# A Strassen–Winograd MLP in another order of its seven products: A12 second, s2 made in the place of s1, other rings for the raw weight blocks

## The chip, the cores and the metric

The kernel runs on one core of one Trainium2 chip. The metric is device time in microseconds of one launch. The kernel before took 734.94 us (median of 3 runs, 733.79 to 735.09). Five engines work in it: TensorE (PE; its weight loads are PEld), VectorE (DVE), ScalarE (ACT), GpSimd (POOL) and SyncE (SP), which issues most transfers. Each engine runs its instructions strictly in its own order; semaphores tie them together.

## The reference

One decoder block in float32 over 512 tokens of width 1024: RMSNorm, an input projection, a pooling mixer and a differential attention mixer, a gated merge and output projection with a residual; cross-attention to 256 memory tokens with a residual; and the MLP, which is what the change touches:

```python
x = x + memory_cross_attention(hc, mem_n, w_cq[l], w_ckv[l], w_co[l])
hm = rms_norm(x, g_mlp[l])                       # D_MODEL 1024, SEQ 512
x = x + jnp.square(jax.nn.relu(hm @ w_up[l])) @ w_down[l]   # D_FF 4096
return rms_norm(x, g_final)
```

## The kernel before

**Float32 by halves.** Every matrix is split into a rounded part and a remainder (`split`: ACT casts the high half, L111; DVE subtracts for the low half, L112), and each product is three matmuls (`mm3`: L105 high by high, L106 high by low, L107 low by high). The right factors lie transposed, 128 rows by 512 tokens.

**Projections.** A projection of width 1024 has 8 output tiles m of 8 x 3 matmuls (128x512). The last one before the MLP is `co` (out of cross-attention). Its tiles run in the order `CO_ORDER` 0 4 1 5 2 6 3 7. `done_co` adds the residual (L573), and `right_factors` makes from tiles m and m+4 the right factors of the MLP's first half: for m < 4, x = g*t (L765, L766, L767), whose halves are B11 and T1; for m >= 4 (L773, L776, L777) the halves B21, B22, T2 and T3; `right_rest` (L791) makes T4. After each tile its square is added to `ss2` (`accumulate`, L263 on ACT, L264 on DVE); when all are there, `ss2` is split (`sp2`) and `stats2`, due `STAT2` steps later, lets PE sum it over the partitions and makes the RMS factor `r2`.

**The MLP's first half** is done in 8 sets n of 512 of the 4096 columns. A set multiplies a 2x2 block matrix by the 2x2 blocks of the right factor with seven block products in the manner of Strassen and Winograd instead of eight. The left factors are the raw blocks A11, A12, A22 and the sums s1 = A21+A22, s3 = A21+A11, s2 = s1+A11 and s4 = s2+A12. A block product is 24 matmuls of 128x256 (`block_product`). `up_set` adds the results in PSUM (tag `sc`, 3 banks) to running sums in SBUF (`plus`, L885), and `squared_relu` (L860, L861, then `split`) turns C11, C12, C21, C22 into right factors for the second half. The result of s1 stays in its bank (`u["P5"]`) until that of s3 is there. Two sets are followed by eight tiles of the second half (`dn`).

**Loads.** `load` fetches a raw block of 128x1024 (512 KB) on SP. s1 and s3 are added in flight: SP fetches one block, then POOL issues an accumulating transfer on top (L164, L167). s2 and s4 are additions on DVE (`combined`, L182 and L185). Raw blocks lie in two rings: `wraw` with 3 buffers, which all other weights use too, and `mraw` with 5, which exists only once the first part's buffers are given back (`renew`, during the first tiles of `co`). `prep` splits a block into a pair of halves (`whi`/`wlo`, 3 pairs, or `mhl`, 2 pairs).

**Order.** PE's order is that of the program. The order on the other engines is made by a scheduler that places instructions by a priority and by its own timeline; `tc.high_priority()` raises it for a block of code. In `done_co` this is done for the last two tiles, 3 and 7.

Of the kernel before, what the change touches and what calls it, by code (L numbers as in the profile page):

```python
# [14 lines left out]
ALU = mybir.AluOpType  # L15
AX = mybir.AxisListType

P = 128
# [14 lines left out]
MEMIN, EARLY, LATE = 16, [4, 5, 6, 0, 1], [2, 7, 3]  # L33
WARM = 8
ON_POOL = (1, 3, 5, 7), (1, 3, 5)
STAT1, STAT2, STATM = 16, 13, 20
CO_ORDER = 0, 4, 1, 5, 2, 6, 3, 7
PARTS = "A11", "A12", "A21", "A22"
ORDER = "A11", "s2", "s1", "s3", "A12", "A22", "s4"
FIRST_ORDER = "A11", "s1", "s2", "A12", "s3", "A22", "s4"  # L40
PLAN = "q0 k0 q1 k1 q2 q3 g4 k2 g5 g6 k3 g7 u0 u1 u2 u3 g0 g1 g2 g3"

G_MIX, G_CROSS, G_MEM, G_MLP, G_FINAL, PSCALE, GSUB, LAMS = 0, 8, 16, 24, 32, 40, 44, 45
# [7 lines left out]
def block_kernel(ctx: ExitStack, tc: tile.TileContext, x0g, xT, memT, wv, wm, wst, wckv, wpool, vecs, csts, outT):  # L51
# [24 lines left out]
    def sb(tag, shape, bufs, dt=F32):  # L76
        p = apool if tag in EARLY_TAGS else late["pool"] if tag in LATE_TAGS else pool
        return p.tile(shape, dt, tag=tag, name=nm(tag), bufs=bufs)
# [67 lines left out]
    def fetch(key, src, tag, bufs):  # L146
        if key not in raw:
            raw[key] = sb(tag, [P, D], bufs)
            nc.sync.dma_start(raw[key], src)
        return raw[key]  # L150

    def part(n, name):
        return wst[4 * n + PARTS.index(name)]

    def load(i):
        if i >= len(blocks):
            return
        if isinstance(blocks[i], tuple):
            n, name = blocks[i]
            if (n, "A11") not in raw:  # L160
                fetch((n, "A11"), part(n, "A11"), "mraw", 5)
            if (n, "s1") not in raw and name in ("s1", "s2"):
                r = fetch((n, "s1"), part(n, "A22"), "wraw", 3)
                nc.gpsimd.dma_start(r, part(n, "A21"), accum_op=ALU.add)  # L164
            if (n, "s3") not in raw and name == "s3":
                r = fetch((n, "s3"), part(n, "A21"), "mraw", 5)
                nc.gpsimd.dma_start(r, part(n, "A11"), accum_op=ALU.add)  # L167
            if name in ("A12", "A22"):
                fetch((n, name), part(n, name), "mraw", 5)
        elif i == 0 and i not in raw:  # L170
            r = raw[i] = sb("wraw", [P, D], 3)
            nc.sync.dma_start(r[:, :T], blocks[i][:, :T])
            load_x(1)
            nc.sync.dma_start(r[:, T:], blocks[i][:, T:])
        else:
            fetch(i, blocks[i], "wraw", 3)

    def combined(n, name):

        if name == "s2":  # L180
            r = raw[n, "s2"] = sb("wraw", [P, D], 3)
            V.tensor_tensor(r, raw[n, "s1"], raw[n, "A11"], op=ALU.add)  # L182
        elif name == "s4":
            r = raw[n, "s2"]
            V.tensor_tensor(r, r, raw[n, "A12"], op=ALU.add)  # L185
            return r
        return raw[n, name]

# [609 lines left out]
    def done_co(m, o):  # L798
        with tc.high_priority() if m in CO_ORDER[-2:] else nullcontext():
            residual(m, o)  # L800
            right_factors(m, res[m])
        accumulate(ss2, m, res[m])
        if m == KC - 1:
            for r in rest:
                right_rest(*r)
# [5 lines left out]
        late["pool"] = ctx.enter_context(tc.tile_pool(name="late", bufs=1))  # L811

    projection("co", cross_o, [0, 1, 2, 3, 4, 5], [6, 7], done_co, renew, CO_ORDER)
    sp2 = split_sq(ss2, T)

    def stats2():
        st["r2"] = rstd_full(sp2, ss2)
# [56 lines left out]
    def up_set(n, act, j0):  # L874

        x, y = ((pair("xg", 8), pair("xg", 8)) for _ in range(2))
        for i in range(2):
            act[j0 + i] = (x[0][:, i, :], x[1][:, i, :])
            act[j0 + 2 + i] = (y[0][:, i, :], y[1][:, i, :])
        u = {}  # L880

        def plus(new, o, old):
            if new not in u:
                u[new] = tmp()
            V.tensor_tensor(u[new], o, u[old], op=ALU.add)  # L885

        for name in FIRST_ORDER if n == 0 else ORDER:
            o = ps("sc", 3)
            block_product(W(n, name), right[RIGHT[name]], o)
            if name == "A11":  # L890
                u["P1"] = tmp()
                S.copy(u["P1"], o)
            elif name == "s2":
                plus("U2", o, "P1")
            elif name == "s1":
                u["P5"] = o
            elif name == "s3":
                plus("U3", o, "U2")
                plus("C22", u["P5"], "U3")
                u["U4"] = u["U2"]  # L900
                plus("U4", u["P5"], "U2")
                squared_relu(*y, u["C22"], B, ALU.min)
            elif name == "A12":
                u["C11"] = u["P1"]
                plus("C11", o, "P1")
                squared_relu(*x, u["C11"], A)
            elif name == "A22":
                u["C21"] = u["U3"]
                plus("C21", o, "U3")
                squared_relu(*y, u["C21"], A, ALU.min)  # L910
            elif name == "s4":
                u["C12"] = u["U4"]
                plus("C12", o, "U4")
                squared_relu(*x, u["C12"], B)
# [110 lines left out]
```

## Time and profile before

| what | us |
|---|---|
| median of 3 runs | 734.94 |
| the profiled execution, its time | 733.65 |
| its span, first to last instruction | 731.7 |
| PE busy in it | 706.8 (97%) |
| DVE busy | 512.7 (70%) |
| ACT busy | 392.4 (54%) |

The page gives busy times by engine, the span in 40 slices, the transfers, the chain of waits that ended last, and the costliest groups of instructions. The timeline gives each instruction with its start, its duration and, in square brackets, the idle time of its engine before it and what ended it. The view by windows gives the busy time of each engine in a stretch, the count of its instructions, the TensorE clock granted by the throttle (1.00 is full) and the share of time in which the 16 DMA engines were busy. A line such as L112 is that of a helper, so the tile's name says what is meant.

### The profile page before, as it was taken

Reading aid. Unit: us, or ns where it says so; the run is one execution under the profiler, and the core shown is the slowest. Engines: PE = TensorE matmul, PEld = TensorE weight load, DVE = VectorE, ACT = ScalarE, POOL = GpSimd, SP = SyncE. Lnnn points to the kernel's source line nnn. Section 1 sums busy time; section 2 is a strip of 40 time slices with the busy share of each in tenths; the row PEclk is TensorE's granted clock in tenths of the full one; section 3 lists DMA queues with packets and bytes.
Section 4 is the critical chain, followed back from the end, with each engine's and each line's share of the span. In section 5 each row is a group of like instructions: output and inputs, shape, how many; then the busy total and the mean of one; then the engine's idle time right before and its main releaser. Section 6 shows DMA issues by size and latency. Waiting matters only on the chain.

```text
span 731.7 us, 10275 instructions
## 1 busy us (share of the span) xinstructions
PE 706.8 (97%) x3960; PEld 614.1 (84%) x3960; DVE 512.7 (70%) x797; ACT 392.4 (54%) x641; POOL 72.6 (10%) x66
## 2 busy tenths in 40 slices
PE   9999999999999999999969999999999999999993
PEld 6877888788889888888849988899889988899882
DVE  7597999975888555663887974588455974489426
ACT  7498998676766433543754641256214651256422
POOL 0044112534000000000000001000000001000003
PEclk9999999999999999999988999999999999999997
DMA  8433223143525542114734646265354645314003
GB/s 318 142 114 117 78 82 115 59 142 119 173 91 186 187 141 87 58 58 159 187 86 122 197 143 144 86 173 184 77 115 146 202 144 118 83 58 144 30 1 115
DMA packets 28112, 91.09 MB, mean 124 GB/s; under 512 B 3072, under 2 KB 5120, under 8 KB 28064
## 3 DMA queue, kind: packets, MB, share of 16 engines
q1 hardware_dynamic: 25712, 81.92, 33.9%
q0 software_dynamic: 2352, 8.52, 6.9%
q8 instruction: 31, 0.51, 0.3%
q14 instruction: 17, 0.14, 0.1%
HBM read 86.24 MB, written 2.10 MB: 121 GB/s over the span
## 4 chain that ended last, share of the span: by engine, by line
PE 81%; DVE 6%; DMA 5%; ACT 5%; issue 1%; POOL 0%; SPq 0%; DVEq 0%; POOLq 0%; ACTq 0%
PE acc L105 16%; PE acc L107 15%; PE acc L106 15%; PE sc L105 10%; PE sc L107 10%; PE sc L106 10%; DMA wraw<-wst 3%; DMA mraw<-wst 2%; DVE wlo L112 1%; ACT tmp L448 1%; ACT whi L111 1%; DVE mix L849 1%; DVE tmp L446 1%; DMA tmp<-xT 1%; PE sc L387 1%
## 5 line engine op out<-in xcount | busy, mean ns | idle before, releaser
L111 ACT CAST whi<-wraw 128x1024 fp32r<-128x1024 f32 (+1 forms) x98 | 102.4, 1045 | 118.1 <-PE acc L106 50.8
L105 PE MATMUL acc<-xg,whi 128*128 128x512 f32 x400 | 158.2, 396 | 0.0
L107 PE MATMUL acc<-xg,wlo 128*128 128x512 f32 x400 | 156.1, 390 | 0.0
L106 PE MATMUL acc<-xg,whi 128*128 128x512 f32 x400 | 155.8, 390 | 0.0
L112 DVE TENSOR_TENSOR wlo<-wraw,whi 128x1024 fp32r<-128x1024 f32 (+1 forms) x98 | 121.3, 1238 | 27.7 <-ACT whi L111 27.4
L107 PEld LDWEIGHTS acc<-xg,wlo 128*128 128x128 f32 x400 | 75.1, 188 | 16.1
L105 PEld LDWEIGHTS acc<-xg,whi 128*128 128x128 f32 x400 | 75.2, 188 | 15.0 <-issue 0.3
L106 PEld LDWEIGHTS acc<-xg,whi 128*128 128x128 f32 x400 | 75.2, 188 | 14.5
L573 DVE TENSOR_TENSOR vr<-acc,vr 128x512 f32<-128x512 f32 x41 | 28.3, 690 | 72.3 <-PE acc L107 72.3
L105 PE MATMUL sc<-mix,whi 128*128 128x256 f32 (+1 forms) x192 | 56.8, 296 | 0.0
L107 PE MATMUL sc<-mix,wlo 128*128 128x256 f32 (+1 forms) x192 | 56.4, 294 | 0.0
L106 PE MATMUL sc<-mix,whi 128*128 128x256 f32 (+1 forms) x192 | 56.4, 294 | 0.0
L885 DVE TENSOR_TENSOR tmp<-sc,tmp 128x512 f32<-128x512 f32 x56 | 37.7, 686 | 7.5 <-PE sc L107 7.3
L111 ACT CAST mhl<-wraw 128x1024 fp32r<-128x1024 f32 x22 | 23.2, 1053 | 35.6 <-PE acc L106 22.2
L111 ACT CAST whi<-mraw 128x1024 fp32r<-128x1024 f32 x19 | 19.9, 1050 | 38.6 <-PE acc L106 21.8
L106 PE MATMUL acc<-xg,mhl 128*128 128x512 f32 x104 | 40.6, 390 | 0.0
L105 PE MATMUL acc<-xg,mhl 128*128 128x512 f32 x104 | 40.5, 389 | 0.0
L107 PE MATMUL acc<-xg,mhl 128*128 128x512 f32 x104 | 40.5, 389 | 0.0
L105 PEld LDWEIGHTS sc<-mix,whi 128*128 128x128 f32 x192 | 36.5, 190 | 1.0
L106 PEld LDWEIGHTS sc<-mix,whi 128*128 128x128 f32 x192 | 36.4, 189 | 1.1
L107 PEld LDWEIGHTS sc<-mix,wlo 128*128 128x128 f32 x192 | 36.4, 190 | 1.1
L167 POOL DMA_DIRECT2D mraw<-wst x8 | 6.9, 864 | 263.5 <-DMA mraw<-wst 164.3
(270 smaller groups left out, 1684.9 us busy)
## 6 DMA issues: line engine op xcount, KB each, us to landing
wraw<-wm SPq DMA_DIRECT2D x76, 512.0 KB, 3.3
mraw<-wst SPq DMA_DIRECT2D x32, 512.0 KB, 3.4
wraw<-wckv SPq DMA_DIRECT2D x16, 512.0 KB, 3.4
mraw<-wst POOLq DMA_DIRECT2D x8, 512.0 KB, 5.7
wraw<-wst SPq DMA_DIRECT2D x8, 512.0 KB, 3.3
wraw<-wst POOLq DMA_DIRECT2D x8, 512.0 KB, 5.6
s<-s SPq DMA_DIRECT2D x8, 256.0 KB, 3.6
vr<-xT SPq DMA_DIRECT2D x8, 256.0 KB, 4.4
```

Of the source, the lines that this page charges most:

```text
L105: nc.tensor.matmul(o, lh, rh, start=start, stop=False)
L106: nc.tensor.matmul(o, lh, rl, start=False, stop=False)
L107: nc.tensor.matmul(o, ll, rh, start=False, stop=stop)
L111: S.copy(hi, src)
L112: eng.tensor_tensor(lo, src, f(hi), op=ALU.subtract)
L167: nc.gpsimd.dma_start(r, part(n, "A11"), accum_op=ALU.add)
L387: nc.tensor.matmul(o[i], xg[k][0][:, tb], wh[:, c], start=k == 0, stop=False)
L446: V.tensor_tensor_reduce(e[:, :n], o[:, :n], mask[:, T - n:], -0.125, 3.0e38, ALU.add, ALU.min, mn)
L448: S.activation(e[:, :n], e[:, :n], AF.Exp, bias=mn, scale=-1.0, accum_out=sm[:, c:c + 1])
L573: V.tensor_tensor(t, o, t, op=ALU.add)
L849: eng.tensor_tensor(y3[j][:, i, c], y3[j][:, i, c], r, op=ALU.mult)
L885: V.tensor_tensor(u[new], o, u[old], op=ALU.add)
```

## The change

The seven products of a set run in the order A11 A12 s1 s2 s3 A22 s4; before, it was A11 s2 s1 s3 A12 A22 s4. In the first set it is A11 s1 A12 s2 s3 A22 s4; before, A11 s1 s2 A12 s3 A22 s4. s2 is formed on DVE in the buffer of s1, where before it had one of its own. The raw s1 moves from the ring `wraw` to the ring `mraw`, and the raw A12 and A22 move from `mraw` to `wraw`. The additions of the squares of the last two `co` tiles and the split of their sum are at high priority too. `STAT2` is 11, before 13. C11 gets a buffer of its own, since A12 is now multiplied while P1 is still needed.

```diff
--- before.py
+++ after.py
@@ -33,11 +33,11 @@
 MEMIN, EARLY, LATE = 16, [4, 5, 6, 0, 1], [2, 7, 3]
 WARM = 8
 ON_POOL = (1, 3, 5, 7), (1, 3, 5)
-STAT1, STAT2, STATM = 16, 13, 20
+STAT1, STAT2, STATM = 16, 11, 20
 CO_ORDER = 0, 4, 1, 5, 2, 6, 3, 7
 PARTS = "A11", "A12", "A21", "A22"
-ORDER = "A11", "s2", "s1", "s3", "A12", "A22", "s4"
-FIRST_ORDER = "A11", "s1", "s2", "A12", "s3", "A22", "s4"
+ORDER = "A11", "A12", "s1", "s2", "s3", "A22", "s4"
+FIRST_ORDER = "A11", "s1", "A12", "s2", "s3", "A22", "s4"
 PLAN = "q0 k0 q1 k1 q2 q3 g4 k2 g5 g6 k3 g7 u0 u1 u2 u3 g0 g1 g2 g3"
 
 G_MIX, G_CROSS, G_MEM, G_MLP, G_FINAL, PSCALE, GSUB, LAMS = 0, 8, 16, 24, 32, 40, 44, 45
@@ -157,16 +157,13 @@
             return
         if isinstance(blocks[i], tuple):
             n, name = blocks[i]
-            if (n, "A11") not in raw:
-                fetch((n, "A11"), part(n, "A11"), "mraw", 5)
-            if (n, "s1") not in raw and name in ("s1", "s2"):
-                r = fetch((n, "s1"), part(n, "A22"), "wraw", 3)
-                nc.gpsimd.dma_start(r, part(n, "A21"), accum_op=ALU.add)
-            if (n, "s3") not in raw and name == "s3":
-                r = fetch((n, "s3"), part(n, "A21"), "mraw", 5)
-                nc.gpsimd.dma_start(r, part(n, "A11"), accum_op=ALU.add)
-            if name in ("A12", "A22"):
-                fetch((n, name), part(n, name), "mraw", 5)
+            if name in ("s1", "s3"):
+                first, then = ("A22", "A21") if name == "s1" else ("A21", "A11")
+                if (n, name) not in raw:
+                    r = fetch((n, name), part(n, first), "mraw", 5)
+                    nc.gpsimd.dma_start(r, part(n, then), accum_op=ALU.add)
+            elif name in PARTS:
+                fetch((n, name), part(n, name), "mraw" if name == "A11" else "wraw", 5 if name == "A11" else 3)
         elif i == 0 and i not in raw:
             r = raw[i] = sb("wraw", [P, D], 3)
             nc.sync.dma_start(r[:, :T], blocks[i][:, :T])
@@ -177,12 +174,9 @@
 
     def combined(n, name):
 
-        if name == "s2":
-            r = raw[n, "s2"] = sb("wraw", [P, D], 3)
-            V.tensor_tensor(r, raw[n, "s1"], raw[n, "A11"], op=ALU.add)
-        elif name == "s4":
-            r = raw[n, "s2"]
-            V.tensor_tensor(r, r, raw[n, "A12"], op=ALU.add)
+        if name in ("s2", "s4"):
+            r = raw[n, "s1"]
+            V.tensor_tensor(r, r, raw[n, "A11" if name == "s2" else "A12"], op=ALU.add)
             return r
         return raw[n, name]
 
@@ -799,7 +793,7 @@
         with tc.high_priority() if m in CO_ORDER[-2:] else nullcontext():
             residual(m, o)
             right_factors(m, res[m])
-        accumulate(ss2, m, res[m])
+            accumulate(ss2, m, res[m])
         if m == KC - 1:
             for r in rest:
                 right_rest(*r)
@@ -811,7 +805,8 @@
         late["pool"] = ctx.enter_context(tc.tile_pool(name="late", bufs=1))
 
     projection("co", cross_o, [0, 1, 2, 3, 4, 5], [6, 7], done_co, renew, CO_ORDER)
-    sp2 = split_sq(ss2, T)
+    with tc.high_priority():
+        sp2 = split_sq(ss2, T)
 
     def stats2():
         st["r2"] = rstd_full(sp2, ss2)
@@ -901,7 +896,6 @@
                 plus("U4", u["P5"], "U2")
                 squared_relu(*y, u["C22"], B, ALU.min)
             elif name == "A12":
-                u["C11"] = u["P1"]
                 plus("C11", o, "P1")
                 squared_relu(*x, u["C11"], A)
             elif name == "A22":
```

The scheduler's order changes with it. On DVE, from the residual of tile 3 of `co` (`vr_1890`) to the low half of its right factor (`mix_3594`), which is the last that the product A11 needs, before (`wraw_3825` is s2 of the second set, `wraw_3670` first s2 and then s4 of the first):

```order
L573 TENSOR_TENSOR vr_1890<-acc_3560,vr_1890 128x512
L112 TENSOR_TENSOR wlo_3673<-wraw_3670,whi_3672 128x1024
L182 TENSOR_TENSOR wraw_3825<-wraw_3711,mraw_3668 128x1024
L112 TENSOR_TENSOR s_3548<-tmp_3545,s_3548 128x512
L767 TENSOR_TENSOR tmp_3593<-tmp_3593,tmp_3595 128x256
L185 TENSOR_TENSOR wraw_3670<-wraw_3670,mraw_3661 128x1024
L264 TENSOR_TENSOR ss_3244<-ss_3244,tmp_3601 128x512
L573 TENSOR_TENSOR vr_1898<-acc_3604,vr_1898 128x512
L791 SCALAR_TENSOR_TENSOR tmp_3545<-tmp_3545,tmp_3542 128x256
L112 TENSOR_TENSOR wlo_3677<-mraw_3661,whi_3676 128x1024
L112 TENSOR_TENSOR mix_3594<-tmp_3593,mix_3594 128x512
```

The same stretch of DVE in the changed kernel (its line numbers are lower by 5 or 6; `mraw_3561` is s1, from here on s2, of the first set, `wraw_3605` is A12):

```order
L567 TENSOR_TENSOR vr_1890<-acc_3560,vr_1890 128x512
L112 TENSOR_TENSOR wlo_3671<-wraw_3605,whi_3670 128x1024
L785 SCALAR_TENSOR_TENSOR tmp_3545<-tmp_3545,tmp_3542 128x256
L761 TENSOR_TENSOR tmp_3593<-tmp_3593,tmp_3595 128x256
L258 TENSOR_TENSOR ss_3244<-ss_3244,tmp_3601 128x512
L112 TENSOR_TENSOR s_3554<-tmp_3545,s_3554 128x256
L567 TENSOR_TENSOR vr_1898<-acc_3604,vr_1898 128x512
L112 TENSOR_TENSOR wlo_3676<-mraw_3561,whi_3675 128x1024
L112 TENSOR_TENSOR mix_3594<-tmp_3593,mix_3594 128x512
```

The two additions of 1024 columns (`wraw_3825`, `wraw_3670`) have left the stretch, `s_3548` now stands just ahead of it, and `s_3554` has come in.

On POOL, the first four accumulating transfers before: s3 of the first and of the second set, then s1 of the first and of the second.

```order
L167 DMA mraw_3663<-wst 128x1024
L167 DMA mraw_3775<-wst 128x1024
L164 DMA wraw_3561<-wst 128x1024
L164 DMA wraw_3711<-wst 128x1024
```

And in the changed kernel: s1 and s3 of the first set, then s1 and s3 of the second.

```order
L164 DMA mraw_3561<-wst 128x1024
L164 DMA mraw_3663<-wst 128x1024
L164 DMA mraw_3741<-wst 128x1024
L164 DMA mraw_3822<-wst 128x1024
```

s1 has moved ahead of s3; its buffer `mraw_3561` is now one of the five that SP fills first when the ring `mraw` comes into being.

On ACT, between the square of tile 3 (`tmp_3601`) and the high half of its right factor (`mix_3594`), before:

```order
L263 ACTIVATE tmp_3601<-vr_1890 128x512
L111 CAST whi_3676<-mraw_3661 128x1024
L111 CAST mix_3594<-tmp_3593 128x512
L773 ACTIVATE tmp_3634<-vr_1898,vx_67 128x512
L111 CAST s_3554<-tmp_3545 128x256
```

and in the changed kernel (`whi_3675` is the high half of s2, before it was that of A12):

```order
L257 ACTIVATE tmp_3601<-vr_1890 128x512
L111 CAST s_3554<-tmp_3545 128x256
L111 CAST whi_3675<-mraw_3561 128x1024
L111 CAST mix_3594<-tmp_3593 128x512
L767 ACTIVATE tmp_3636<-vr_1898,vx_67 128x512
```

`s_3554` has moved ahead; a cast of a weight block still stands right ahead of `mix_3594`.

## The prediction, made before the change was run

> **What bounds the kernel now.** First the page:
>
> ```profile
> span 731.7 us, 10275 instructions
> PE 706.8 (97%) x3960; PEld 614.1 (84%) x3960; DVE 512.7 (70%) x797; ACT 392.4 (54%) x641; POOL 72.6 (10%) x66
> ```
>
> PE is the bound. An edit on other engines pays only where PE stands still or runs at a lower clock, so I asked the view by windows where that is (columns: us, PE busy, PEld, DVE, ACT, POOL, granted clock, DMA share, GB/s):
>
> ```profile
> 54.00:58.00 4.00, 2.42 (x13) 2.02 (x13) 2.63 (x5) 2.24 (x5) 2.56 (x2) 1.00 0.62 186
> 336.00:375.00 39.00, 39.00 (x173) 32.06 (x172) 28.73 (x45) 23.31 (x38) 3.46 (x4) 1.00 0.70 193
> 376.40:378.50 2.10, 0.00 (x0) 0.00 (x0) 1.04 (x1) 0.32 (x1) 0.00 (x0) 1.00 0.21 39
> 378.50:378.70 0.20, 0.00 (x0) 0.00 (x0) 0.20 (x2) 0.00 (x0) 0.00 (x0) 0.71 0.00 0
> 384.09:388.70 4.61, 4.61 (x21) 4.61 (x22) 3.53 (x8) 2.05 (x3) 0.00 (x0) 0.50 0.35 114
> 388.70:389.00 0.30, 0.30 (x4) 0.30 (x3) 0.30 (x1) 0.30 (x2) 0.00 (x0) 0.80 0.00 0
> 410.00:700.00 290.00, 290.00 (x1827) 262.60 (x1826) 193.30 (x230) 123.13 (x152) 9.48 (x11) 1.00 0.44 124
> ```
>
> From 410 to 700, where nearly all of the eight sets lie, PE is busy without a gap: the new order of products can gain nothing there, only lose. The gap that the change can touch lies at the first product, between `co` and the MLP. There the clock also falls to 0.50 and stays so for 4.6 us after PE is back at work. PE's timeline there:
>
> ```profile
> 374.70 0.39 PE L106 MATMUL acc<-xg,whi 128*128 128x512 f32 x1
> 374.93 0.39 PE L107 MATMUL acc<-xg,wlo 128*128 128x512 f32 x1
> 375.15 0.28 PE L105 MATMUL sc<-mix,mhl 128*128 128x256 f32 x1
> 376.10 0.28 PE L107 MATMUL sc<-mix,mhl 128*128 128x256 f32 x1
> 380.33 0.58 PE L105 MATMUL sc<-mix,mhl 128*128 128x256 f32 x1 [3.95 <-ACT mix L111]
> 384.09 0.58 PE L106 MATMUL sc<-mix,mhl 128*128 128x256 f32 x1 [3.18 <-DVE mix L112]
> ...
> 388.90 0.28 PE L107 MATMUL sc<-mix,wlo 128*128 128x256 f32 x1
> 390.67 0.28 PE L107 MATMUL sc<-mix,wlo 128*128 128x256 f32 x1
> 390.78 0.28 PE L105 MATMUL sc<-s,whi 128*128 128x256 f32 x1
> ```
>
> A11 starts at 375.15, does the nine matmuls of k = 0 to 2, and then lacks the right factor of k = 3 (`mix`, from tile 3 of `co`): its high half from ACT until 380.33, its low half from DVE until 384.09. At full clock a matmul comes every 0.118 us (388.90 to 390.67 in 15 steps). The third product starts 48 matmuls after the first, so without a hitch it would start at 375.15 + 48 x 0.118 = 380.8; it starts at 390.78. **10.0 us are lost here**, and no more can be won. Why the factor is late, DVE's timeline tells:
>
> ```profile
> 353.61 1.29 DVE L112 TENSOR_TENSOR mix<-tmp,mix 128x512 fp32r<-128x512 f32 x2
> 361.50 0.68 DVE L573 TENSOR_TENSOR vr<-acc,vr 128x512 f32<-128x512 f32 x1
> 364.60 1.23 DVE L182 TENSOR_TENSOR wraw<-wraw,mraw 128x1024 f32<-128x1024 f32 x1 [2.42 <-DMA wraw<-wst]
> ...
> 373.64 0.68 DVE L573 TENSOR_TENSOR vr<-acc,vr 128x512 f32<-128x512 f32 x1
> 374.24 1.21 DVE L112 TENSOR_TENSOR wlo<-wraw,whi 128x1024 fp32r<-128x1024 f32 x1
> 377.46 1.23 DVE L182 TENSOR_TENSOR wraw<-wraw,mraw 128x1024 f32<-128x1024 f32 x1 [2.01 <-DMA wraw<-wst]
> 378.61 0.68 DVE L112 TENSOR_TENSOR s<-tmp,s 128x512 fp32r<-128x512 f32 x1
> 379.21 0.42 DVE L767 TENSOR_TENSOR tmp<-tmp,tmp 128x256 f32<-128x256 f32 x1
> 379.54 1.22 DVE L185 TENSOR_TENSOR wraw<-wraw,mraw 128x1024 f32<-128x1024 f32 x1
> 380.68 0.69 DVE L264 TENSOR_TENSOR ss<-ss,tmp 128x512 f32<-128x512 f32 x1
> 381.28 0.68 DVE L573 TENSOR_TENSOR vr<-acc,vr 128x512 f32<-128x512 f32 x1
> 381.88 0.42 DVE L791 SCALAR_TENSOR_TENSOR tmp<-tmp,tmp 128x256 f32<-128x256 f32 x1
> 382.21 1.22 DVE L112 TENSOR_TENSOR wlo<-mraw,whi 128x1024 fp32r<-128x1024 f32 x1
> 383.35 0.68 DVE L112 TENSOR_TENSOR mix<-tmp,mix 128x512 fp32r<-128x512 f32 x1
> ```
>
> Twice an s2 addition stands in DVE's queue and waits for the accumulating transfer that makes s1 (2.42 and 2.01 us), with the factor's own work queued behind it; L185 (s4) stands there too. PE had finished tile 3 of `co` some 5.5 us before tile 7, near 369.9 (24 matmuls of 0.227 us), but its residual came at 373.64. From the rows, DVE takes one step of 1024 columns per 1.14 us, of 512 per 0.60, of 256 per 0.33.
>
> **The change part by part.** *Both waits go.* s1 of the first and second set now lie in buffers that SP fills first in the new ring, and POOL adds onto s1 first of all:
>
> ```profile
> 349.58 1.05 ACT L111 CAST mhl<-mraw 128x1024 fp32r<-128x1024 f32 x1 [1.21 <-DMA mraw<-wst]
> 375.69 1.03 ACT L111 CAST whi<-mraw 128x1024 fp32r<-128x1024 f32 x1
> 344.20 0.88 POOL L167 DMA_DIRECT2D mraw<-wst  x1 [162.39 <-DMA mraw<-wst]
> 356.58 0.86 POOL L167 DMA_DIRECT2D mraw<-wst  x1 [11.50 <-DVE tmp L767]
> 358.27 0.86 POOL L164 DMA_DIRECT2D wraw<-wst  x1 [0.84 <-DVE ss L264]
> ```
>
> POOL's first accumulation was issued at 344.20 and used at 349.58. s1 now takes that place, some 20 us before DVE needs it near 366.
>
> *DVE up to tile 3.* From 361.50 to the residual of tile 3 the new queue holds three steps of 1024, eight of 512, six of 256 columns: 3.4 + 4.8 + 2.0 = 10.2, so 371.7 in place of 373.64. (Against before: 2.42 of waiting less, one step of 512 more.)
>
> *DVE from there to the factor*, by the order shown: residual to 372.3; low half of A12 to 373.5; L791's step 373.8; L767's 374.15 (its inputs from ACT come some 1.3 after the residual, at 373.5); the square 374.75; a 256-step 375.1; then the residual of tile 7, whose PE product ends at 374.93 + 0.39 = 375.32, to 375.95. The low half of s2 needs its high half from ACT, whose buffer pair is free when L106 of tile 7 ends (374.70 + 0.39 = 375.1): cast 375.15 to 376.2 (1.03 in the row at 375.69). So DVE does it from 376.2 to 377.35 and the factor's low half to 377.35 + 0.68 = 378.05. The factor's high half follows the cast on ACT: 376.2 + 0.6 = 376.8.
>
> *PE.* It arrives at k = 3 at 376.2, gets the high half at 376.8 and the low half at **378.1**, where it had 384.09. After that matmul 38 remain to the third product: 378.1 + 38 x 0.118 = 382.6, against 390.78. **Gain 8.2**: 6.0 from the stall, 2.2 from the clock, if that holds.
>
> *The squares at high priority.* The one of tile 3 (0.60) lies ahead of the factor, but in the time in which DVE would wait for tile 7 anyway (375.1 to 375.35); without that cover it would cost up to 0.35. Before, it lay there as well.
>
> *What is late next.* `STAT2` 11 puts the sum over `ss2` 18 matmuls into the third product, 382.6 + 2.1 = 384.7. In the changed DVE queue the low half of `ss2` stands nine steps behind the factor's; eight steps lie between (two of 1024, three of 512, three of 256): 377.95 + 2.3 + 1.8 + 1.0 = 383.05, and done at 383.7, 1.0 before PE wants it. I take nothing; what DVE is later than that 1.0, PE waits. The other factors of tile 7 are due later: the low half for A12 at about 380.4 against 383.7.
>
> *Steady state.* In each set the s1 result now blocks its bank over two products, s2 and s3, so A22 must start in the bank of s2. The addition that frees it (L885, 0.69) has the 24 x 0.118 = 2.8 us of product s3 to run in. DVE is 67% busy from 410 to 700 (193.3 of 290), so I take nothing. Loads: as many of each kind; each has a product's time or more between the release of its buffer and its use. C11's own buffer: no work added. Nothing too.
>
> *Unknown: the first accumulations.* s3 of the first set is now second. Its cast heads ACT's queue at 349.58, with the first factors behind it. Bound below: it lands as before, and the DVE run, which no longer starts behind it, gains up to 0.7, useless since the factor hangs on tile 7. Two accumulations in a row are in the trace: issued at 356.58 and 358.27, the second was in use 6.3 after issue (364.60). With that, s3 lands at 350.5 to 351.5, its casts (1.05 and 1.14) end by 353.7, level with 353.61: no shift. Bound above: s3 starts only when s1 has ended; s1, whose block is fetched one place earlier, issued about 1 us before 344.20, and 5.4 for each (344.20 to 349.58): 343 + 2 x 5.4 = 353.8, casts to 356.0, a shift of 2.4. The residual of tile 7 then waits for DVE, 377.5 in place of 375.35, and the low half comes at 379.9. I take the middle one, whose row is the nearest.
>
> *The clock* is priced on the rows: 0.71 in 378.50:378.70 puts the fall at 378.58, 2.2 us after PE stopped; 0.80 in 388.70:389.00 puts the rise at 388.82. The fall came with 1.2 us of work in the 3.4 us before it. In 54.00:58.00 PE stood 1.58 us and kept 1.00:
>
> ```profile
> 55.63 0.33 PE L444 MATMUL sc<-s,s 128*128 128x128 f32 x1 [1.58 <-DMA s<-s]
> ```
>
> The new stall is 0.4 + 1.0 us with a matmul between, nearer to that row. I take no fall. The Trainium skill (TensorE: Matmul & The Clock Gate, "What's actually happening") has a free-running window of 3413 ns and a fall after at least one idle window. The 10.24 us at 0.50 are three such windows; that the window must be idle throughout, the trace contradicts, since PE had been idle for 2.2 us only. By the page's wording the fall would have no chance here.
>
> **The sum.** Span 731.7 - 8.2 = 723.5. The profiled execution took 733.65, 1.95 more than its span: 725.4. The median lies 1.3 above it, 734.94: **726.7 us**.
>
> **The rivals.** (a) *The clock falls all the same.* For: where the window lies is chance, and half of one could be idle. Against: the row at 55.63. It costs what the row 384.09:388.70 shows, half of 4.6 less a little, 2.1: gain 6.1, 728.8. (b) *The first accumulations collide* (bound above). For: DMA share 0.70 from 336 to 375, and a third accumulation and a `co` load fall into the same time. Against: the pair at 356.58. Low half at 379.9, third product 384.4, gain 6.4; PE then stands over 3 us and the clock most likely falls: 4.3, 730.6. (c) *Slower: the bank of s2.* If DVE, queued behind casts of weights that wait for PE, adds U2 later than 2.8 us after s2, PE stops before A22 in all eight sets. It decides from 2.8 + 8.2/8 = 3.8 us of lag per set; at 5 us the loss is 8 x 2.2 = 17.6 against 8.2: 744.3. For: three banks, one held longer. Against: DVE's idle third. (d) *The change does not do what it says*: the factor is late for another reason, such as ACT's cast of s2 in front of it waiting for a load that is still late, and the stall stays: 734.9.
>
> **How the numbers follow.** Forecast (gain 7 to 10) 0.62; (a) 0.15; (b) 0.12; (c) 0.06; (d) 0.02; small gains otherwise 0.03. Within the forecast 725.0 (all 10.0) to 728. The range takes in (a) and (b): 725.0 to 730.8, with (c) and (d) left out. 0.2%, 1.5 us, is about what a measurement tells from no change: faster 0.91, same 0.03, slower 0.06.
>
> **What would show it.** Right: no wait of DVE for a transfer between 360 and 380; PE's waits at the first product below 2 us in all; clock 1.00 until the tail; third product some 7.5 us after the first. Wrong: a wait of PE on an addition L885 (880 in the changed file) in the sets; the casts of s3 after 354; the sum over `ss2` waiting for its split; clock 0.50 near 380.

## The result: 727.16 us, 1.1% faster, and what the profile after shows

The changed kernel takes 727.16 us (median of 5, 726.64 to 728.78) against 735.09 (5 runs, 733.79 to 736.44): ratio 0.9887, 95% interval 0.9874 to 0.9900. 726.7 was forecast. The profiled execution took 726.64 us, its span is 724.9 (before: 733.65 and 731.7).

PE's timeline at the first product of the changed kernel (columns as before: start, duration, engine, line, operation, and in brackets the idle time and what ended it):

```profile
375.42 0.28 PE L105 MATMUL sc<-mix,mhl 128*128 128x256 f32 x1
...
377.01 0.39 PE L105 MATMUL sc<-mix,mhl 128*128 128x256 f32 x1 [0.37 <-ACT mix L111]
378.35 0.38 PE L106 MATMUL sc<-mix,mhl 128*128 128x256 f32 x1 [0.96 <-DVE mix L112]
...
382.93 0.28 PE L105 MATMUL sc<-mix,whi 128*128 128x256 f32 x1
...
385.05 0.39 PE L231 MATMUL tr<-tmp,ones 128*128 128x512 f32 x1
```

The two waits for the factor of k = 3 are 0.37 and 0.96 us, where they were 3.95 and 3.18. The matmul behind the second takes 0.38 us, where it took 0.58: the clock stays at 1.00, and falls only in the tail. The third product starts 382.93 - 375.42 = 7.51 us after the first; before it was 390.78 - 375.15 = 15.63. So 8.12 us were gained at this place.

Why, DVE's timeline of the changed kernel shows, and beside it the view of DVE's waits from 360 to 395 us (columns: who waits for whom, us in all, times, longest), first of before, then of after:

```profile
371.53 0.70 DVE L567 TENSOR_TENSOR vr<-acc,vr 128x512 f32<-128x512 f32 x1
...
375.62 0.69 DVE L567 TENSOR_TENSOR vr<-acc,vr 128x512 f32<-128x512 f32 x1 [0.65 <-PE acc L107]
376.47 1.23 DVE L112 TENSOR_TENSOR wlo<-mraw,whi 128x1024 fp32r<-128x1024 f32 x1 [0.16 <-ACT whi L111]
377.61 0.69 DVE L112 TENSOR_TENSOR mix<-tmp,mix 128x512 fp32r<-128x512 f32 x1
...
383.30 0.68 DVE L112 TENSOR_TENSOR tmp<-ss,tmp 128x512 fp32r<-128x512 f32 x1
```

```profile
DVE wraw L182 <- DMA wraw<-wst: 4.4, 2, 2.4
```

```profile
DVE vr L567 <- PE acc L107: 0.6, 1, 0.6
DVE tmp L880 <- PE sc L107: 0.6, 1, 0.6
DVE wlo L112 <- ACT whi L111: 0.4, 2, 0.3
```

The waits for the accumulating transfer of s1 are gone, no other of their size came, and the residual of tile 7 (375.62) now waits for PE, the engine that should set the pace. From 386 us to the tail PE waits for nothing.

The span is only 6.8 us shorter, not 8.1. A11 starts 0.27 later than before, and from the third product to the tail the changed kernel takes 1.04 longer (the start of the last tile less that of the third product: 711.74 - 390.78 = 320.96 before, 704.93 - 382.93 = 322.00 after). That is no wait but a pace of the matmuls, told at the end.

### The profile page after: what moved, and what is told of

It is laid out like the page before. It is cut to its first block, busy times and chain, and to the rows that moved or that the text cites. A ratio compares the mean times of both kernels' runs of the same rounds, so it can differ in the third digit from the quotient of the medians.

```text
span 724.9 us, 10273 instructions
## 1 busy us (share of the span) xinstructions
PE 705.0 (97%) x3960; PEld 613.3 (85%) x3960; DVE 513.5 (71%) x797; ACT 391.8 (54%) x641; POOL 72.6 (10%) x66
## 4 chain that ended last, share of the span: by engine, by line
PE 87%; DVE 5%; ACT 4%; DMA 1%; issue 1%; POOL 0%; SPq 0%; DVEq 0%; ACTq 0%
PE acc L105 17%; PE acc L106 17%; PE acc L107 17%; PE sc L105 10%; PE sc L106 10%; PE sc L107 10%; ACT tmp L442 1%; DVE mix L844 1%; ACT whi L111 1%; DMA tmp<-xT 1%; DVE tmp L440 1%; PE sc L381 1%; DVE wlo L112 1%; ACT tmp L412 1%; PE sc L383 1%
## 5 line engine op out<-in xcount | busy, mean ns | idle before, releaser
L111 ACT CAST whi<-wraw 128x1024 fp32r<-128x1024 f32 (+1 forms) x93 | 97.0, 1044 | 106.9 <-PE acc L106 40.2
L112 DVE TENSOR_TENSOR wlo<-wraw,whi 128x1024 fp32r<-128x1024 f32 (+1 forms) x93 | 115.3, 1241 | 28.7 <-ACT whi L111 28.2
L164 POOL DMA_DIRECT2D mraw<-wst x16 | 13.8, 862 | 429.3 <-DMA mraw<-wst 353.5
L105 PE MATMUL sc<-mix,whi 128*128 128x256 f32 (+1 forms) x184 | 54.3, 295 | 0.0
L107 PE MATMUL sc<-mix,wlo 128*128 128x256 f32 (+1 forms) x184 | 54.1, 294 | 0.0
L106 PE MATMUL sc<-mix,whi 128*128 128x256 f32 (+1 forms) x184 | 54.1, 294 | 0.0
L111 ACT CAST whi<-mraw 128x1024 fp32r<-128x1024 f32 x24 | 25.0, 1051 | 45.6 <-PE acc L106 33.0
L880 DVE TENSOR_TENSOR tmp<-sc,tmp 128x512 f32<-128x512 f32 x56 | 37.7, 689 | 6.6 <-PE sc L107 6.4
L111 ACT CAST mhl<-wraw 128x1024 fp32r<-128x1024 f32 x19 | 20.0, 1052 | 35.2 <-PE acc L106 18.0
L107 PEld LDWEIGHTS sc<-mix,wlo 128*128 128x128 f32 x184 | 34.6, 188 | 1.1
L105 PEld LDWEIGHTS sc<-mix,whi 128*128 128x128 f32 x184 | 34.6, 188 | 1.0
L106 PEld LDWEIGHTS sc<-mix,whi 128*128 128x128 f32 x184 | 34.5, 187 | 1.1
```

Source lines behind the costliest of these rows:

```text
L105: nc.tensor.matmul(o, lh, rh, start=start, stop=False)
L106: nc.tensor.matmul(o, lh, rl, start=False, stop=False)
L107: nc.tensor.matmul(o, ll, rh, start=False, stop=stop)
L111: S.copy(hi, src)
L112: eng.tensor_tensor(lo, src, f(hi), op=ALU.subtract)
L164: nc.gpsimd.dma_start(r, part(n, then), accum_op=ALU.add)
```

## The experiments

Two theories stood against each other. **T**: the transfer that makes s1 comes late, since its buffer lay in a ring behind the weights of `co`, and DVE's queue stands behind it; the new rings cure that. **Rivals**: the order of the products alone does it (fewer or later additions in DVE's queue); the priority of the squares does it. Ratios are to runs of the kernel before on the same chip.

**1. The squares alone.** On the kernel before:

```diff
-STAT1, STAT2, STATM = 16, 13, 20
+STAT1, STAT2, STATM = 16, 11, 20
         with tc.high_priority() if m in CO_ORDER[-2:] else nullcontext():
             ...
-        accumulate(ss2, m, res[m])
+            accumulate(ss2, m, res[m])
-    sp2 = split_sq(ss2, T)
+    with tc.high_priority():
+        sp2 = split_sq(ss2, T)
```

> The kernel before with one part of the change alone: the squares of the last two tiles and the split of their sum at high priority, and STAT2 at 11; products and buffers as before, so both additions that make s2 (and the one that makes s4) still stand in VectorE's queue ahead of tile 3's factor. If the late accumulating transfer in front of the factor is the cause (theory): no gain, 734 to 736 us, PE again without work for 7 us at the first product (before: 3.95 + 3.18) and the clock at 0.50 after it. If the squares' place did it (rival): both waits fall below 2 us in all and the time comes near 727.

735.07 us, ratio 1.0011 (0.9996 to 1.0025): no gain. PE waits 3.6 and 3.4 us at the first product. The other way round, the changed kernel without these priorities:

> The changed kernel without the priority of the last squares and of the split of their sum (STAT2 stays at 11). VectorE's order from tile 3's residual to the factor is the changed one but for the square. Theory: the squares cost and give nothing at the first product: 727.2 us within 0.2%; the sum over ss2 in the third product waits for its split, at most 1 to 2 us. Rival (the squares' priority carries a part of the gain): 729 us or more.

727.76 us, ratio 0.9916 (0.9889 to 0.9942); PE's waits there 0.37 and 1.22. No wait came at the sum over `ss2`, which the theory had allowed for. The priority is no measurable part of the gain, and it costs nothing that shows.

**2. The order of the products without the new rings.** On the changed kernel, s1 goes to the ring `wraw` again, A12 and A22 to `mraw`:

```diff
-                    r = fetch((n, name), part(n, first), "mraw", 5)
+                    r = fetch((n, name), part(n, first), *(("wraw", 3) if name == "s1" else ("mraw", 5)))
...
-                fetch((n, name), part(n, name), "mraw" if name == "A11" else "wraw", 5 if name == "A11" else 3)
+                fetch((n, name), part(n, name), "mraw", 5)
```

> The changed kernel with the buffers as they were: s1 again in the ring of three, behind the weights of co; A12 and A22 in the ring of five. The order of the products and VectorE's order of work in the stretch are the changed ones, and the addition of s2 of the second set does not stand there. Theory (s1's transfer is late because of its ring): the first set's s1 lands near 364.6 as before, VectorE waits some 2.4 us for it, the residual of tile 3 comes at some 374 in place of 371.5, the low half of its factor at some 380.2 in place of 378.35, PE waits some 3 us in all: 729.0 if the clock stays, 731 if it falls. Rival (the order of products alone gives the gain, the rings do nothing): 727 us, PE's waits 1.3 us in all.

734.58 us, ratio 1.0002 (0.9984 to 1.0019): nothing is left of the gain. Yet neither theory had it right, for the stall is gone. POOL issues the first set's accumulation as late as before (there it was 358.27), and DVE adds s2 without a wait; the timelines of POOL and DVE of this kernel:

```profile
360.04 0.86 POOL L164 DMA_DIRECT2D wraw<-wst  x1 [13.33 <-DVE ss L258]
```

```profile
370.64 1.22 DVE L179 TENSOR_TENSOR wraw<-wraw,mraw 128x1024 f32<-128x1024 f32 x1
```

In the new order s2 is the fourth product, so its addition stands later in the queue (370.64, where L182 was reached at 362.2 and waited until 364.60), and that of the second set has left the stretch. PE waits 0.4 and 1.0 us at the first product, and the first set takes 22.11 us, as in the changed kernel. The time is lost again in the down-projections. PE's timeline, and the view by windows over the first and third pair of sets' down-projection (us, PE busy, PEld, DVE, ACT, POOL, clock, DMA share, GB/s):

```profile
425.64 0.50 PE L105 MATMUL acc<-xg,mhl 128*128 128x512 f32 x1 [1.31 <-ACT xg L111]
...
593.70 0.50 PE L105 MATMUL acc<-xg,whi 128*128 128x512 f32 x1 [0.70 <-ACT xg L111]
...
595.33 0.50 PE L106 MATMUL acc<-xg,whi 128*128 128x512 f32 x1 [1.12 <-DVE xg L112]
```

```profile
418.70:464.36 45.66, 44.12 (x195) 35.96 (x193) 23.48 (x27) 11.94 (x14) 1.71 (x2) 1.00 0.39 108
587.40:634.94 47.54, 45.72 (x194) 37.07 (x193) 24.40 (x29) 12.16 (x15) 1.72 (x2) 0.96 0.37 105
```

The same two stretches take 43.66 and 43.56 us in the changed kernel. With the second (43.86 against 43.56) and the start of A11 (376.80 against 375.42) that is 2.0 + 4.0 + 0.3 + 1.4 = 7.7, all of the difference of the spans (732.6 - 724.9). The 1.4 lie ahead of the MLP, in an execution whose clock also fell at 56.95, and nothing in the trace ties them to the edit. Behind the 4.0 stands a weight of the down-projection that came late; ACT's timeline, then DVE's:

```profile
585.30 1.05 ACT L111 CAST mhl<-wraw 128x1024 fp32r<-128x1024 f32 x1 [4.10 <-DMA wraw<-wm]
```

```profile
586.38 1.23 DVE L112 TENSOR_TENSOR mhl<-wraw,mhl 128x1024 fp32r<-128x1024 f32 x1 [3.77 <-ACT mhl L111]
587.52 1.28 DVE L880 TENSOR_TENSOR tmp<-sc,tmp 128x512 f32<-128x512 f32 x2
```

The low half of that weight stands in DVE's queue ahead of the last additions of the set (L880), and they stand ahead of the squared activations for which PE then waits; in the third pair the clock falls too. It is the pattern that the first product had before, in another place. The chain of waits has the transfer itself (start, duration):

```profile
577.51 7.71 DMA wraw<-wm
```

It is the third of the eight weights. SP issued it, right behind four raw blocks, 9.9 us before the down-projection starts (587.37), and it was not there until 585.22. In the changed kernel the third weight was issued 12.2 us before the start (571.50 against 583.68) and was there after 6.2.

**3. The new rings without the order.** On the kernel before:

```diff
-                r = fetch((n, "s1"), part(n, "A22"), "wraw", 3)
+                r = fetch((n, "s1"), part(n, "A22"), "mraw", 5)
...
-                fetch((n, name), part(n, name), "mraw", 5)
+                fetch((n, name), part(n, name), "wraw", 3)
```

> The kernel before with the new buffers alone: s1 in the ring of five, A12 and A22 in the ring of three beside s2, the products in the old order. Theory (the late s1 is the cause): no wait of VectorE for a transfer between 360 and 380; the additions of s2 (first set) and s4 still stand ahead of the factor and cost 1.14 each, so the residual of tile 3 comes at some 371.5 and the low half of tile 3's factor at 378 to 379.5: 727 to 729 us, unless the ring of three, which now serves s2 too, makes PE wait in the sets. Rival (the order of the products is what counts, the additions in the queue keep the factor late): PE waits over 4 us in all at the first product, the clock falls, 731 to 735 us.

729.61 us, ratio 0.9932 (0.9909 to 0.9955). T holds here: DVE waits for no transfer between 360 and 395, though the additions still stand ahead of the factor, and PE waits 1.23 us. But 2.4 us more than the changed kernel's span remain, and most of them lie in the second set and the down-projection behind it. PE's timeline, ACT's and DVE's:

```profile
378.85 0.38 PE L106 MATMUL sc<-mix,mhl 128*128 128x256 f32 x1 [1.23 <-DVE mix L112]
...
415.47 0.36 PE L105 MATMUL sc<-mix,whi 128*128 128x256 f32 x1 [1.36 <-DVE tmp L885]
```

```profile
412.41 1.05 ACT L111 CAST mhl<-wraw 128x1024 fp32r<-128x1024 f32 x1 [4.30 <-DMA wraw<-wm]
```

```profile
413.50 1.23 DVE L112 TENSOR_TENSOR mhl<-wraw,mhl 128x1024 fp32r<-128x1024 f32 x1 [2.87 <-ACT mhl L111]
414.64 1.88 DVE L885 TENSOR_TENSOR tmp<-sc,tmp 128x512 f32<-128x512 f32 x3
```

Again ACT waits for a weight `wm`, whose low half stands at the head of DVE's queue, and behind it the addition that frees a bank (L885). But this one was not issued late; it landed slowly, as the chain of waits has it:

```profile
404.78 7.56 DMA wraw<-wm
```

It is the second weight. The changed kernel issued its second at 404.58, and it landed after 4.8 us. **So each half of the change lifts the stall by itself, and each alone pays for it in the sets; only both together keep the whole gain.** Why this transfer was slow, and why the other one was issued late, stays open.

**4. Tile 3 ahead of tile 6.** `CO_ORDER = 0, 4, 1, 5, 2, 3, 6, 7`, first on the changed kernel, then on the kernel before.

> The changed kernel with the last three tiles of co in the order 3 6 7 in place of 6 3 7. What is left of the stall after the change is 0.37 + 0.96 us at k = 3 of the first product, and the factor there hangs on tile 3, whose steps stand on VectorE and ACT beside those of tile 7. If tile 3 is done one tile (5.4 us) earlier, its factor is ready before PE asks, and both waits go: 725.8 us. Rival: the wait moves to the next product that needs tile 6 or 7 (A12, 24 matmuls or 2.8 us later), since VectorE has the same work ahead of it: 727 us, no change.

> The kernel before with the same order of tiles, 3 6 7 in place of 6 3 7, and nothing else. The two additions of s2 still wait for their transfers (2.42 and 2.01 us) in VectorE's queue. Theory: tile 3's factor comes before the second of the waits and no longer stops the first product, but what hangs on tile 7 in the second product (2.8 us later) still comes late behind the second wait: a part of the gain, 729 to 732 us. Rival (the place of tile 3 is all that matters, the additions could have stayed): 727 us or less.

On the changed kernel 726.84 us, ratio 0.9900 (0.9883 to 0.9917): no difference from the change as it was. The waits at k = 3 are gone, but one came at the sum over `ss2`, whose split DVE ends only at 384.81. PE's timeline of it:

```profile
384.87 0.50 PE L232 MATMUL tr<-tmp,ones 128*128 128x512 f32 x1 [1.06 <-DVE tmp L112]
```

On the kernel before: 735.93, ratio 1.0018 (1.0007 to 1.0028), not better, where T promised a part of the gain. DVE waits as before, and PE stands in the third product, which starts at 381.85, instead of the first (the expectation had the second); DVE's timeline, then PE's:

```profile
365.65 1.23 DVE L182 TENSOR_TENSOR wraw<-wraw,mraw 128x1024 f32<-128x1024 f32 x1 [2.83 <-DMA wraw<-wst]
...
378.48 1.23 DVE L182 TENSOR_TENSOR wraw<-wraw,mraw 128x1024 f32<-128x1024 f32 x1 [2.32 <-DMA wraw<-wst]
```

```profile
385.10 0.38 PE L106 MATMUL sc<-s,whi 128*128 128x256 f32 x1 [2.27 <-DVE s L112]
...
388.20 0.58 PE L105 MATMUL sc<-s,whi 128*128 128x256 f32 x1 [2.60 <-ACT s L111]
...
390.52 0.58 PE L106 MATMUL sc<-s,whi 128*128 128x256 f32 x1 [1.74 <-DVE s L112]
```

6.6 us of waiting and the fall of the clock, as before. The wait in DVE's queue is the cause, not tile 3's place.

**5. The sum over `ss2` later** (`STAT2` 12, with tile 3 ahead of tile 6), beside the changed kernel once more.

> The changed kernel with the tiles of co in the order 3 6 7 and STAT2 at 12 in place of 11: the sum over ss2 comes six matmuls (0.71 us) later, behind the third product. With the tiles alone PE's waits at the first product went and one of 1.06 us for the split of ss2 came. Theory (only that split is then late): 0.4 us of waiting is left, the first set takes some 20.9 us in place of 22.1, 726.0 us, or 1.2 below the changed kernel on the same chip. Rival (VectorE is simply that much behind, and what comes after the sum, the reciprocal root for the first squared relu, is late in its turn): PE waits 1 us or more later in the set, 727.0 us.

> The changed kernel once more, unaltered, for two questions. First, beside the version with tile 3 ahead of tile 6 and the sum over ss2 later, on the same chip. Second, the pace of the 128x256 matmuls: the profiled execution of the changed kernel has 117.8 ns a matmul in all eight sets, that of the kernel before had 113.3 in the rest of the first and in the second set (1.0 us together). If the pace belongs to the program, all sets show 117.8 again; if it belongs to the execution, it may be 113.3 in some. Time 727.2 either way, within 0.2%.

727.22 us (725.99 to 729.01) against 727.59 (726.7 to 732.14): the rival's answer. In the trace the first set takes 21.11 us in place of 22.11, and the next set and its down-projection give the 1.0 back (19.96 + 44.50 against 19.79 + 43.66). From 396.5 to 408 DVE is busy without a gap. That reads as DVE's backlog: a PE that is earlier meets it later. It is not fully shown, for only 0.37 of the 1.0 are waits of PE (0.15 and 0.22, at the down-projection).

**6. More work for DVE.** Tile 3's factor gets three or six more steps (`V.tensor_scalar(x, x, 1.0, None, op0=ALU.mult)`).

> The changed kernel with three more steps of 512 columns on VectorE (some 0.60 each, values unchanged) in the making of tile 3's factor: 1.8 us of delay added where the new version has 0.65 us of waiting for tile 7. Prices lateness of VectorE after the change. If PE's stall takes the delay one to one and the clock stays: the stall goes from 1.33 to about 2.5 and the time from 727.2 to 728.4. If the clock falls already at such a stall: 2.1 more, 730.5.

> As the one with three steps, with six: 3.6 us of delay. One to one and the clock stays: stall some 4.3 us, 730.2. With the fall of the clock, which the kernel before had at 3.95 + 3.18 us: 732.3, with the granted clock at 0.50 near 380. Which of the two tells how near the changed kernel is to the fall.

732.13 (ratio 0.9965, 0.9952 to 0.9977) and 733.0 (0.9979, 0.9966 to 0.9991), both above what was expected even with a fall of the clock (730.5 and 732.3). A step with one input took 0.33 us from start to start, not 0.60, so only 1.0 us was added by the three; but the scheduler also put the low half of s2's weight (1.2) and tile 7's residual between them, and s4's addition (L179, 1.1) ahead of the factor's low half. And in the profiled execution tile 3's residual came 1.6 us later (373.12 against 371.53) before any added step, since the transfer of s3 landed 1.6 later (its cast at 352.77 against 351.19). So its stall is not the price of three steps alone. PE's timeline with three steps:

```profile
380.04 0.58 PE L105 MATMUL sc<-mix,mhl 128*128 128x256 f32 x1 [3.10 <-ACT mix L111]
381.74 0.58 PE L106 MATMUL sc<-mix,mhl 128*128 128x256 f32 x1 [1.12 <-DVE mix L112]
```

The stall is 4.2 us, the clock falls at 379.83 for 6.83 us, and the first set takes 5.3 us more (27.40 against 22.11): 2.9 of stall and 2.4 of clock. With six steps s3 was in time (351.07), PE waits 4.96 and 0.14 us, and the clock falls as well. The clock and the pace of the matmuls, told at the end, rest also on a second execution of the kernel before, unaltered:

> The kernel before once more, unaltered, one look, for the pace alone. If 113.3 ns a matmul from 394 to 424 us and in the memory keys belongs to the program, both stretches show it again; if to the execution, one of them or both show 117.8, and the profiled span grows by up to 1.0 (sets) and 0.4 (keys).

735.65 us, with 3.44 and 3.18 us of waiting at the first product.

**7. The squares' additions on GpSimd**, with tile 3 ahead of tile 6:

```diff
-    def accumulate(ss, k, src, w=T):
+    def accumulate(ss, k, src, w=T, eng=V):
...
-            V.tensor_tensor(ss, ss, sq, op=ALU.add)
+            eng.tensor_tensor(ss, ss, sq, op=ALU.add)
...
-            accumulate(ss2, m, res[m])
+            accumulate(ss2, m, res[m], eng=G)
```

> The changed kernel with the tiles of co in the order 3 6 7 (STAT2 at 11) and the seven additions of the squares of co's tiles (0.60 us each on VectorE) on GpSimd, which has only four transfers to issue between 340 and 390 us. Theory (what is left of the stall is VectorE's backlog, 4.2 us of which leave its queue): the split of ss2 is done by 383.4, PE waits nowhere in the first two sets for more than 0.3 us in all, the first set takes 20.4 us (170 matmuls of 0.118 and the slower pair of the sum) in place of 22.1, and the clock cannot fall at the first product: 725.6 us. Rival (the wait hangs on the chain through ACT, or GpSimd takes as long for its additions, 1.3 us each, as the sum can wait): PE still waits 1 us at the sum, 726.8 us, the same as with the tiles alone.

731.6 us, ratio 0.9963 (0.9948 to 0.9978): 4.4 us slower than the changed kernel, which neither side expected. POOL's timeline, DVE's and PE's:

```profile
378.52 1.41 POOL L258 TENSOR_TENSOR ss<-ss,tmp 128x512 f32<-128x512 f32 x1 [3.30 <-ACT tmp L257]
384.28 2.23 POOL L258 TENSOR_TENSOR ss<-ss,tmp 128x512 f32<-128x512 f32 x1 [4.35 <-ACT tmp L257]
```

```profile
378.10 0.68 DVE L112 TENSOR_TENSOR mix<-tmp,mix 128x512 fp32r<-128x512 f32 x1
378.92 1.56 DVE L112 TENSOR_TENSOR s<-tmp,s 128x512 fp32r<-128x512 f32 x1
...
384.17 1.22 DVE L179 TENSOR_TENSOR mraw<-mraw,wraw 128x1024 f32<-128x1024 f32 x1
385.31 1.75 DVE L112 TENSOR_TENSOR mix<-tmp,mix 128x512 fp32r<-128x512 f32 x1
```

```profile
387.12 0.58 PE L106 MATMUL sc<-mix,whi 128*128 128x256 f32 x1 [2.98 <-DVE mix L112]
```

While POOL adds, a DVE step of 512 columns takes 1.56 and 1.75 us in place of 0.68. The step of 1024 (L179), which had begun at 384.17, just before POOL's addition at 384.28, kept its 1.22; there it is POOL's addition that took 2.23 in place of 1.41. What leaves DVE's queue (0.60) comes back as some 0.9 to 1.1 of standing in these two steps, and as 1.7 in one of 256 columns (2.14 us at 361.70 in place of 0.42). PE waits 2.98 us in the third product, and the clock falls.

## Why the prediction was right, and where it was not

| step, as predicted | predicted | measured |
|---|---|---|
| both waits of DVE for s1's transfer | gone | gone |
| residual of tile 3 | 371.7 | 371.53 |
| first accumulation of s3: cast | 350.5 to 351.5 | 351.19 |
| its accumulating transfer, from issue to use | 6.3 | 7.7 |
| residual of tile 7 | 375.35 | 375.62 (A11 is 0.27 later) |
| factor of k = 3, high half | 376.8 | 376.95 |
| its low half | 378.05 | 378.30 |
| PE resumes | 378.1 | 378.35 |
| split of `ss2` done, PE wants it | 383.7, 384.7 | 383.98, 385.05 |
| third product after the first | 7.45 | 7.51 |
| gain there | 8.2 | 8.12 |
| span | 723.5 | 724.9 |
| median | 726.7 | 727.16 |

**DVE's steps.** The sum of steps by their width, 10.2 us from one residual to the next, came out at 371.53 - 361.31 = 10.22. As long as the queue waits for nothing, it can be added up.

**What was wrong: the cause of the missing waits.** The prediction laid them to the rings ("s1 of the first and second set now lie in buffers that SP fills first"). That happens, but the run with the old rings shows it isn't needed: with s1's accumulation issued at 360.04, the new order alone has the addition 6 us later in the queue and the second set's out of the stretch. Both parts widen the same distance, from the transfer to the addition that needs it.

**"Steady state: nothing"** is right for the change as a whole and hides what the rings are for. With the order alone the down-projections lost 6.3 us; with the rings alone the second set and its down-projection lost 2.3. The pattern of the slower rival, an addition that frees a bank and stands behind the work on a weight, did occur with the rings alone, in the old order of products, at 1.36 us once, and not in the changed kernel.

**The squares** cost nothing and gave nothing, as forecast; the margin of 1.0 at `ss2` was 1.07.

**The clock, and the first accumulations.** "I take no fall" held in the profiled execution and was a narrow thing. Its evidence was the row at 55.63, a stall of 1.58 us without a fall. As the last part shows, what counts is the idle time within one window of 3.41 us, and there a window happened to begin at 54.32, so that only 1.32 us of the stall lay in it. At the same place the clock did fall in two other executions (at 56.95 with the old rings, at 58.38 in the repeated run), so the row was luck. The repeated run caught one slower execution among six: 732.14 us, the other five from 726.7 to 727.94 with a mean granted clock of 0.993 to 0.995. Two rivals are in it: (a), the fall of the clock, and in part (b), accumulations that collide. ACT's wait for the transfer of s3, in the changed kernel's first profile and in this one:

```profile
351.19 1.05 ACT L111 CAST mhl<-mraw 128x1024 fp32r<-128x1024 f32 x1 [0.83 <-DMA mraw<-wst]
356.38 1.05 ACT L111 CAST mhl<-mraw 128x1024 fp32r<-128x1024 f32 x1 [2.21 <-DMA mraw<-wst]
```

Counted from A11 (375.42 and 379.23) s3 is 1.4 us later there, tile 3's residual too (376.74), and DVE no longer waits for PE at tile 7's. The stall was 0.40 + 1.32 in place of 0.37 + 0.96, the clock fell, and the third product came 9.44 us after the first, 1.9 more than 7.51; (a) was priced at 2.1. The other 3.8 us of this execution lie ahead of A11: 1.86 ahead of PE's 60th matmul and 1.95 from there on, a stretch that holds the fall at 58.38.

**Two numbers came out right by luck.** s3's transfer took 7.7 us from issue to use (7.7 to 8.6 in eight executions that have both the new order and the new rings), not 6.3; the forecast of its cast held because it was issued at 343.50, and the forecast was a range. And the median missed by only 0.5 us because two errors cancel: the span was forecast 1.4 too short, and the way from span to median was taken as 1.95 + 1.3 = 3.25 us, where it was 727.16 - 724.9 = 2.26.

**The mis-sized term** is that of the span: 1.4 us, of which 0.08 is the place itself, 0.27 lies ahead of A11 and 1.04 in the pace of the matmuls, which the prediction took as one number (0.118 us) for both kernels.

## What to carry to other kernels

An operation in an in-order queue that waits for an accumulating transfer holds up all that stands behind it; move it away from its transfer by either end, by an earlier buffer or by a later use, and look at what the freed ring now delays. After such a repair, ask what the next bound is before repairing on: here it was, as far as the traces show, VectorE's backlog: neither another order of tiles nor a later sum moved the median, and GpSimd made it worse. Keep a stall well below the size at which the clock falls, not only below the size of the stall that was there.

## What the runs showed of the hardware that was not expected

**When the clock falls.** In all executions the changes of the granted clock lie on a grid of 3.413 us: in one execution of the changed kernel it falls at 58.38 and at 382.65, which are 95.0 such windows apart, and it stays at 0.50 for 3.41, 6.83 or 10.24 us. What decides is PE's busy share in the window that ends there. The views by windows show it, each row from the start to the end of one window (the second number after the stretch is PE's busy time). The kernel before, with a fall behind the window:

```profile
375.17:378.58 3.41, 1.21 (x10) 1.00 (x8) 1.40 (x2) 1.55 (x3) 0.00 (x0) 1.00 0.51 100
```

The changed kernel, with none:

```profile
376.66:380.08 3.42, 2.12 (x15) 1.92 (x16) 3.42 (x6) 2.69 (x5) 0.00 (x0) 1.00 0.00 0
```

Its repeated execution, with a fall at the end of the first row:

```profile
379.24:382.65 3.41, 1.69 (x12) 1.29 (x10) 3.41 (x6) 3.38 (x6) 0.00 (x0) 1.00 0.00 0
382.65:386.06 3.41, 3.41 (x16) 3.41 (x17) 3.41 (x6) 1.06 (x3) 0.00 (x0) 0.50 0.22 44
```

The changed kernel with the old rings, with a fall behind each row:

```profile
53.54:56.95 3.41, 1.80 (x11) 1.37 (x10) 2.00 (x5) 2.54 (x6) 2.43 (x2) 1.00 0.81 232
592.85:596.26 3.41, 1.59 (x6) 0.97 (x6) 2.66 (x5) 2.02 (x4) 0.00 (x0) 1.00 0.66 243
```

The kernel before with the squares alone, with none:

```profile
53.50:56.90 3.40, 1.79 (x11) 1.38 (x10) 1.99 (x5) 2.76 (x6) 1.95 (x2) 1.00 0.85 230
```

And the kernel before with tile 3 ahead of tile 6, with a fall:

```profile
382.54:385.95 3.41, 0.79 (x5) 0.38 (x3) 3.41 (x5) 2.57 (x4) 0.00 (x0) 1.00 0.15 35
```

It fell behind 1.21, 1.69, 1.80, 1.59 and 0.79 us of work, and not behind 2.12. At 1.8 it is a toss: it fell behind the 1.80 of the old rings, not behind the 1.79 of the squares alone. Over fourteen profiled executions, past their first 15 us, every full-clock window with 1.7 us or more of idleness was followed by a fall, and none with 1.59 or less. In between, from 1.60 to 1.62, it fell behind one window of six. So 1.7 us without work in one window is enough, 1.6 can be, and the changed kernel's 1.30 has little room. The Trainium skill (TensorE: Matmul & The Clock Gate, "What's actually happening") calls the window free-running and 3413 ns long, and the traces agree; that it takes an idle window, they contradict: half of one did.

**Two paces of the same matmuls.** A set of 168 matmuls of 128x256 without a wait takes 19.79 us (117.8 ns each) in nearly all sets, but 19.04 (113.3 ns) in the second set of the kernel before. PE's timeline, the set's first matmul and the first of the down-projection, of before and of after:

```profile
404.98 0.28 PE L105 MATMUL sc<-mix,whi 128*128 128x256 f32 x1
...
424.02 0.39 PE L105 MATMUL acc<-xg,mhl 128*128 128x512 f32 x1
```

```profile
397.53 0.28 PE L105 MATMUL sc<-mix,whi 128*128 128x256 f32 x1
...
417.31 0.39 PE L105 MATMUL acc<-xg,mhl 128*128 128x512 f32 x1
```

The pace begins behind the two matmuls of the sum over `ss2` and ends at the down-projection or at a wait. It came in both profiled executions of the kernel before, with the squares alone, with the new rings alone, with six steps, and in the repeated execution of the changed kernel; in its first one and in all the others not. Five of these six, all but that of the new rings, had a fall of the clock just before, but three executions with a fall there or in the next product (three steps, tile 3 first on the kernel before, squares on GpSimd) kept to 117.8. The memory keys near 230 us ran at 113.3 in one execution of the kernel before and at 117.8 in the other, so it is not the program alone that sets it. What does stays open; at 4.5 ns a matmul it hid 1.0 us of the gain between the two profiled executions.

**GpSimd beside VectorE.** The additions on POOL stretched DVE's steps from 0.68 to 1.56 and 1.75 us. The Trainium skill (GPSIMD Engine Reference, "1. Specifications") names contention for VectorE's instructions with two inputs from SBUF; those stretched here have two. Not every such step was stretched: L179 above has two as well and was not.

**The start.** PE's 60th matmul starts between 17.45 and 19.50 us in the fourteen profiled executions, at 17.75 and 19.50 in the two of the kernel before and at 17.63 and 19.49 in the two of the changed kernel. Up to 2 us of the difference between two single times lie there; the cause is open.
